# Layer 2's first forget gates set behind the second tile's splitting, and the first experts' last combinations in another order

## The chip, the cores and the metric

The kernel runs on one core of one Trainium2 chip. The metric is the device time of one execution in microseconds (us), the median of three timed runs. One more execution was taken with the hardware profiler; every row quoted here is from it.

## What is computed

The reference sends 256 tokens of width 1024 through two transformer blocks in fp32. The first has two layers (attention, a short convolution), each with a dense feed-forward part. The second has a layer with the HGRN2 mixer and one with stick-breaking attention, each followed by a normalisation over the residual sum, a mixture of 16 experts and another normalisation. What the change touches is the forget gate of the HGRN2 mixer and the output of the first mixture:

```python
def second_block(x, mem, ...):
    ...
    for layer in range(DEPTH):
        ...
            h = x @ a_w_in[layer]
            q, f_raw, i_in, g, qm = jnp.split(h, [...], axis=-1)
            seq_out = hgrn2_mix(q, f_raw, i_in, g, lb_all[layer], a_gnorm[layer])
        ...
        x = post_norm(x, mixed @ w_o[layer], ln_mix_g[layer], ln_mix_b[layer])
        moe_out = hier_moe(x, w_group[layer], b_group[layer], ...)
        x = post_norm(x, moe_out, ln_ffn_g[layer], ln_ffn_b[layer])
    return x

def hgrn2_mix(q, f_raw, i_in, g, lb, gnorm):
    ...
    logf = jnp.logaddexp(jnp.log(lbf), jnp.log1p(-lbf) + jax.nn.log_sigmoid(f_raw))
    kh = -jnp.expm1(logf)
    vh = i_in...
    o = gla_chunkwise(qh, kh, vh, logf)   # S_t = diag(f_t) S_{t-1} + k_t^T v_t ; o_t = q_t S_t
    ...

def hier_moe(x, ...):
    ...                                    # top group, then the top 2 of its 4 experts
    h = jax.nn.silu(einsum('td,edf->tef', xf, w_gate)) * einsum('td,edf->tef', xf, w_up)
    y = einsum('tef,efd->td', h * gates[:, :, None], w_down)
    return y
```

## The kernel before

The 256 tokens are two tiles T of 128 (0 and 1, `x_82` and `x_83` in the order, both x in the trace). A dense product is made of three matmuls in a reduced fp32 format: the weight is split into hi (cast by ScalarE, L506, now and then by VectorE, L502) and lo (subtracted by VectorE, L487), and so is the activation. A weight unit is 128 x 1024 and 512 KB; one tile needs six matmuls of 128 x 512 for it.

Nothing is ordered by hand. A planner runs generators of work (one per tile and side task) against its own clock, and writes out the order of each engine and of the DMA queue. A generator yields what it waits for: a named event, banks of PSUM, free buffers, or a priority. `rS(n)` asks for n of the 34 places of a ring of 128 x 1024 buffers, which holds activations, weights as they come from memory (raw) and their hi and lo. `SMIN` is the number of places that are always counted as taken by activations: `can_dma` lets a new unit be loaded, and `hl_max` lets units be split ahead, only within what is left.

Layer 2 is the projection of HGRN2. For each tile `lhsT` transposes x on TensorE (L464) and splits it; `gemm` takes blocks of 512 columns, and each block has a callback that spends its bank (b0 to b6). b0 and b1 spawn `f_part`, the forget gates: Abs, Exp and Ln on ScalarE (L480, L484), two scalings on VectorE (L498), then Exp and the cast on ScalarE, and the subtraction of the rest on VectorE. The Exp needs its table loaded (L470). b2 spawns `hgrn`, the recurrence: it waits for both parts of the gates, transposes k and q (twelve matmuls, L464), and sets up the decays with products against a constant matrix.

In `moe_task` the experts stand in four groups of slots, q = 0 to 3, and two column halves c. `down(q, c)` is the down product of both tiles, scaled into two buffers (ScalarE L480, VectorE L498). `combined(q, c)` adds it into the tiles' output banks with four matmuls. For q = 3 the two tiles are apart: `down_last(T, c)` (eight matmuls; the trace has two records for each) and `combined_last(T, c)` (two matmuls). Then `moe` takes the statistics of the output bank (L2152), the residual and the gain are applied in four VectorE operations (L498, x<-bk,stat,row), x is transposed, split, and the next layer's product begins. Layer 0 of `moe_task` is the first mixture.

Of the kernel before, what the change touches and what calls it, by code (L numbers as in the profile page):

```python
# [301 lines left out]
class Body:  # L302
# [1092 lines left out]
    def layer2(self, T):  # L1395
        if T == 0:
            self.hv, self.gs, self.ktil = {}, {}, None
            self.SMIN, self.RAWMIN = 19, 2
        yield self.rS(2)
        lhs = self.pair()  # L1400
        ev = self.lhsT(T, self.x[T], lhs, at=self.ut[T])
        lfh = lfl = kk = qq = vv = gs = mm = None
        mix = []

        def a0():
            nonlocal lfh, lfl, kk
            lfh, lfl, kk = self.tS(F32R), self.tS(F32R), self.tS()

        def a1():
            nonlocal qq  # L1410
            qq = self.tS()

        def a3():
            nonlocal vv
            vv = self.hv[T] = self.tS()

        def a4():
            nonlocal gs
            gs = self.gs[T] = self.tS()

        def f_part(acc, c, d, ev, last=True):
            n = d.stop - d.start
            yield self.rH(2)
            t1, t2 = self.tH(), self.tH()
            self.act(t1[:, :n], acc[:, c], AF.Abs)
            self.act(t1[:, :n], t1[:, :n], AF.Exp, scale=-1.0)
            self.act(t1[:, :n], t1[:, :n], AF.Ln, bias=1.0)
            yield self.w()
            self.stt(t2[:, :n], acc[:, c], 0.0, t1[:, :n], ALU.max, ALU.add)
            self.stt(t1[:, :n], acc[:, c], 0.0, t1[:, :n], ALU.min, ALU.subtract)  # L1430
            if last:
                self.free()
            self.act(kk[:, d], t2[:, :n], AF.Exp, scale=-1.0)
            self.scopy(lfh[:, d], t1[:, :n])
            yield self.w()
            self.tt(lfl[:, d], t1[:, :n], lfh[:, d].bitcast(F32), ALU.subtract)
            self.fH(2)
            self.set(ev)

        def b0(acc):  # L1440
            self.sch.spawn(f_part(acc, slice(0, 512), slice(0, 512), f"lf{T}_0"), 0)

        def b1(acc):
            self.scopy(qq[:, :256], acc[:, 256:])
            self.sch.spawn(f_part(acc, slice(0, 256), slice(512, 768), f"lf{T}_1"), 0)

        def b2(acc):
            self.scopy(qq[:, 256:768], acc)
            self.free()
            self.sch.spawn(self.hgrn(T, lfh, lfl, kk, qq, mix), 0)  # L1450

        def b3(acc):
            self.act(vv[:, :512], acc, AF.Copy, scale=128.0 ** -0.5)
            self.free()

        def b4(acc):
            self.act(vv[:, 512:768], acc[:, :256], AF.Copy, scale=128.0 ** -0.5)
            self.set(f"hv{T}")
            self.act(gs[:, :256], acc[:, 256:], AF.Silu)
            self.free()  # L1460

        def b5(acc):
            self.act(gs[:, 256:768], acc, AF.Silu)
            self.free()
            self.set(f"hg{T}")

        def b6(acc):
            nonlocal mm
            qm, mm = self.tH(), self.tH(F32R)
            self.scopy(qm[:, :256], acc[:, :256])  # L1470
            self.free()
            self.sch.spawn(self.mem_attention(T, 0, qm, mm), 0)

        u = self.ids["ain"]
        yield from self.gemm(T, u[:24], lhs, [(b0, 3, a0), (b1, 1, a1), b2, (b3, 1, a3), (b4, 1, a4), b5], ev=ev)
        yield from self.gemm(T, u[24:], lhs, [b6], n=256)
        self.fS(2)
        mix += self.pair()
        self.set(f"mix{T}")
        yield f"hgrn{T}"  # L1480
        yield from self.wo_postnorm(T, 0, mix, mm)
# [477 lines left out]
    def moe_task(self, layer):  # L1959
# [11 lines left out]
        def combine(q, c):  # L1971
            for T in range(2):
                if out[T][c] is None:
                    out[T][c] = self.bank()
                for p in range(2):
                    self.mm(out[T][c], self.selT[:, T * 512 + q * 128:T * 512 + (q + 1) * 128],
                            ys[q, c][p][:, T * 512:(T + 1) * 512], q == 0 and p == 0, False)
            self.fS(2)
# [67 lines left out]
        def down(q, c):  # L2046
            ud = self.ids[f"ed{layer}"][8 * q + 4 * c:8 * q + 4 * c + 4]
            yield [f"hT{layer}_{q}_0", f"hT{layer}_{q}_1", f"gsl{layer}", self.rS(2), self.bk(2)] + [self.unit(u) for u in ud]
            y = [self.bank(), self.bank()]
            ys[q, c] = (self.tS(F32R), self.tS(F32R))  # L2050
            ws = [self.take(u) for u in ud]
            for j in range(2):
                for T in range(2):
                    for e in range(4):
                        self.mm(y[T][32 * e:32 * e + 32], hTs[q][:, T * 256 + j * 128 + 32 * e:T * 256 + j * 128 + 32 * e + 32],
                                ws[e][:, j * 512:(j + 1) * 512], j == 0, j == 1)
            for u in ud:
                self.done(u)
            if c:
                self.fH()  # L2060
            for T in range(2):
                n = slice(T * 512, (T + 1) * 512)
                g = gsl[:, 4 * T + q:4 * T + q + 1]
                self.act(ys[q, c][0][:, n], y[T], AF.Copy, scale=g)
                self.stt(ys[q, c][1][:, n], y[T], g, ys[q, c][0][:, n].bitcast(F32), ALU.mult, ALU.subtract)
                self.free()
            self.set(f"y{layer}_{q}_{c}")

        def down_last(T, c):

            ud = self.ids[f"ed{layer}"][24 + 4 * c:28 + 4 * c]
            yield [f"hT{layer}_3_{T}", f"gsl{layer}", self.bk(1)] + [self.unit(u) for u in ud] + ([] if c else [self.rS(2)])
            y = self.bank()
            if c == 0:
                ys[3, T] = (self.tS(F32R), self.tS(F32R))
            ws = [self.take(u) for u in ud]
            for j in range(2):
                for e in range(4):
                    self.mm(y[32 * e:32 * e + 32], hTs[3][:, T * 256 + j * 128 + 32 * e:T * 256 + j * 128 + 32 * e + 32],
                            ws[e][:, j * 512:(j + 1) * 512], j == 0, j == 1)  # L2080
            if T:
                for u in ud:
                    self.done(u)
            n = slice(c * 512, (c + 1) * 512)
            g = gsl[:, 4 * T + 3:4 * T + 4]
            self.act(ys[3, T][0][:, n], y, AF.Copy, scale=g)
            self.stt(ys[3, T][1][:, n], y, g, ys[3, T][0][:, n].bitcast(F32), ALU.mult, ALU.subtract)
            self.free()
            self.set(f"yl{layer}_{T}_{c}")

        def combined_last(T, c):
            yield f"yl{layer}_{T}_{c}"
            for p in range(2):
                self.mm(out[T][c], self.selT[:, T * 512 + 384:T * 512 + 512], ys[3, T][p][:, c * 512:(c + 1) * 512], False, p == 1)
            self.sch.set(f"moe{layer}_{T}_{c}")
            if c:
                self.fS(2)

        def combined(q, c):
            yield [f"y{layer}_{q}_{c}"] + ([f"selT{layer}_0", f"selT{layer}_1", self.bk(2)] if q == 0 else [])  # L2100
            combine(q, c)
# [10 lines left out]
        for q in range(3):  # L2112
            yield from down(q, 0)
            if q > 1:
                yield from combined(q - 1, 1)
            yield from down(q, 1)
            yield from combined(q, 0)
            if q < 2:
                yield from gate_up(q + 2, (0, 1))
            if q == 0:  # L2120
                yield from combined(0, 1)
                yield from residual(0)
                yield from residual(1)
        self.hold = True
        yield from down_last(0, 0)
        yield from combined(2, 1)
        yield from down_last(0, 1)
        yield from down_last(1, 0)
        yield from combined_last(0, 0)
        yield from combined_last(0, 1)  # L2130
        yield from down_last(1, 1)
        yield from combined_last(1, 0)
        self.fH(2)
# [153 lines left out]
```

## Time and profile before

| | |
|---|---|
| median of three runs | 1202.5 us (1201.07 to 1202.95) |
| the profiled execution | 1199.67 us |
| its span in the trace | 1197.9 us |
| TensorE matmuls busy | 1143.5 us (95%) |
| VectorE busy | 726.8 us (61%) |
| ScalarE busy | 545.9 us (46%) |
| DMA, mean over the span | 252 GB/s |

The span is read from the first to the last instruction in the trace; 1.8 us of the profiled execution lie around it. The busy shares are means over stages with different limits, so a stage is read by itself: in its timeline, the number in brackets behind a row is the idle time of the engine before it, and the name after it is what released the engine. Idle time counts only where the engine that sets the pace has it.

### The profile page before, as it was taken

How to read it: one execution, taken by the hardware profiler on the slowest of the kernel's cores; microseconds unless marked ns; L12 is line 12 of the kernel's file. 1: busy time of each engine (PE TensorE's matmuls, PEld its weight loads, DVE VectorE, ACT ScalarE, POOL GpSimd, SP SyncE). 2: the span in 40 equal slices, each digit the busy share in tenths (PEclk: the TensorE clock that was granted, in tenths of full speed). 3: DMA queues.
4: the chain of work that ended last, by engine and by line, in shares of the span. 5: the costliest groups of instructions: out<-in, count | busy, mean ns of one | idle time of the engine just before them, and what ended most of it. 6: DMA issues, size and time to landing. Idle time of an engine off the chain costs nothing. (4 is left out here: it accounts for less than half of the span.)

```text
span 1197.9 us, 16678 instructions
## 1 busy us (share of the span) xinstructions
PE 1143.5 (95%) x6344; PEld 819.6 (68%) x6344; DVE 726.8 (61%) x1126; ACT 545.9 (46%) x908; POOL 44.7 (4%) x65
## 2 busy tenths in 40 slices
PE   7999989999998999999999999999999899999995
PEld 4777768888886777788887789886333577673331
DVE  4577667667577987665556567768121765564214
ACT  4555465434436455544434484554121456631211
POOL 0021000000000000000000000100000100000001
PEclk9999999999999999999999999999999899999997
DMA  9976768777674966566665332577999742587993
GB/s 373 409 287 248 261 216 293 277 262 257 256 271 137 331 227 211 179 208 202 208 224 179 122 124 71 176 255 280 400 409 409 289 153 75 187 333 311 409 408 148
DMA packets 83544, 301.72 MB, mean 252 GB/s; under 512 B 9408, under 2 KB 9824, under 8 KB 83456
## 3 DMA queue, kind: packets, MB, share of 16 engines
q1 hardware_dynamic: 82224, 298.37, 68.9%
q0 software_dynamic: 944, 1.82, 0.5%
q8 instruction: 52, 0.85, 0.3%
q10 hardware_dynamic: 288, 0.38, 0.1%
q14 instruction: 36, 0.29, 0.1%
HBM read 298.83 MB, written 2.10 MB: 251 GB/s over the span
## 5 line engine op out<-in xcount | busy, mean ns | idle before, releaser
L452 PE MATMUL bk<-hi,tS 128*128 128x512 f32 (+1 forms) x1760 | 586.2, 398 | 14.7 <-ACT hi L506 8.5
L452 PEld LDWEIGHTS bk<-hi,tS 128*128 128x128 f32 x1760 | 331.6, 189 | 87.7 <-ACT hi L506 8.9
L487 DVE TENSOR_TENSOR lo<-raw,hi 128x1024 fp32r<-128x1024 f32 x266 | 317.3, 1221 | 53.3 <-ACT hi L506 51.2
L452 PE MATMUL bk<-lo,tS 128*128 128x512 f32 (+1 forms) x880 | 344.1, 391 | 1.6 <-DVE lo L487 1.6
L506 ACT CAST hi<-raw 128x1024 fp32r<-128x1024 f32 x262 | 263.0, 1049 | 8.5 <-DMA raw<-in_units_dram 7.3
L452 PEld LDWEIGHTS bk<-lo,tS 128*128 128x128 f32 x880 | 167.1, 190 | 34.9 <-DVE lo L487 3.4
L480 ACT ACTIVATE tH<-bk 128x256 f32<-128x256 f32 (+1 forms) x100 | 44.8, 449 | 267.4 <-PE bk L452 267.3
L452 PE MATMUL bk<-hi,tH 128*128 128x512 f32 x384 | 132.6, 395 | 1.4 <-ACT tH L506 1.4
L487 DVE TENSOR_TENSOR tH<-tH,bk 128x256 f32<-128x256 f32 x60 | 25.1, 418 | 144.0 <-ACT tH L480 144.0
L452 PE MATMUL bk<-raw,tB 128*32 128x512 f32 x768 | 92.5, 595 | 0.2 <-DMA raw<-in_units_dram 0.2
L452 PEld LDWEIGHTS bk<-hi,tH 128*128 128x128 f32 x384 | 71.9, 188 | 16.9 <-ACT tH L506 2.1
L452 PE MATMUL bk<-raw,tH 128*32 128x512 f32 x640 | 82.2, 595 | 0.6 <-DMA raw<-in_units_dram 0.5
L452 PE MATMUL bk<-lo,tH 128*128 128x512 f32 x192 | 74.9, 390 | 0.0
L498 DVE SCALAR_TENSOR_TENSOR tS<-raw,cs,tS 128x1024 f32<-128x1024 f32 x52 | 66.5, 1279 | 0.3
L452 PEld LDWEIGHTS bk<-raw,tB 128*32 128x32 f32 x768 | 23.8, 110 | 53.4 <-issue 45.2
L498 DVE SCALAR_TENSOR_TENSOR tS<-bk,gsl,tS 128x512 fp32r<-128x512 f32 x32 | 23.3, 748 | 56.1 <-ACT tS L480 55.8
L464 PE MATMUL bk<-identr,tH 128*128 128x128 f32 x296 | 49.9, 277 | 6.8 <-DVE tH L487 3.0
L452 PEld LDWEIGHTS bk<-raw,tH 128*32 128x32 f32 x640 | 21.6, 109 | 49.6 <-issue 40.2
L464 PEld LDWEIGHTS bk<-identr,tH 128*128 128x128 f32 x296 | 35.8, 140 | 28.7 <-issue 8.8
L480 ACT ACTIVATE tS<-bk,gsl 128x512 fp32r<-128x512 f32 x32 | 21.1, 686 | 61.4 <-PE bk L452 61.4
L506 ACT CAST tH<-bk 128x256 fp32r<-128x256 f32 (+1 forms) x52 | 18.5, 356 | 66.4 <-PE bk L464 63.0
L487 DVE TENSOR_TENSOR tH<-bk,tH 128x256 fp32r<-128x256 f32 (+1 forms) x52 | 20.8, 400 | 45.3 <-ACT tH L506 45.2
(198 smaller groups left out, 994.6 us busy)
## 6 DMA issues: line engine op xcount, KB each, us to landing
raw<-in_units_dram SPq DMA_DIRECT2D x556, 512.0 KB, 5.6
row<-in_rows_dram SPq DMA_DIRECT2D x9, 512.0 KB, 7.8
x<-in_x_dram SPq DMA_DIRECT2D x2, 512.0 KB, 9.0
xsave<-x POOLq DMA_DIRECT2D x2, 512.0 KB, 6.2
out_dram<-x SPq DMA_DIRECT2D x3, 256.0 KB, 2.2
ulv<-in_ulv_dram POOLq DMA_DIRECT2D x1, 384.0 KB, 7.2
cst<-in_consts_dram SPq DMA_DIRECT2D x1, 274.0 KB, 10.9
out_dram<-x ACTq DMA_DIRECT2D x1, 256.0 KB, 2.1
```

Source lines behind the costliest of these rows:

```text
L452: self.nc.tensor.matmul(out, lhsT, rhs, start=start, stop=stop, skip_group_check=shared)
L464: self.nc.tensor.transpose(out, in_, self.ident)
L480: self.nc.scalar.activation(out, in_, func, scale=scale)
L487: self.nc.vector.tensor_tensor(out, a, b, op)
L498: self.nc.vector.scalar_tensor_tensor(out, a, s, b, op0, op1)
L506: self.nc.scalar.copy(out, a)
```

## The change

In layer 2 `SMIN` starts at 13 instead of 19, and goes to 19 when the third block of either tile is done. The forget gates of tile 0 wait for the event `lhs2`, which tile 1 sets when the second half of its x is transposed and split. In the first mixture (layer 0; the second is as before) `combined(2, 0)` goes behind `down_last(0, 0)`, `combined(2, 1)` behind `down_last(0, 1)`, and `down_last(1, 0)` behind both `combined_last` of tile 0.

```diff
     def layer2(self, T):
         if T == 0:
             self.hv, self.gs, self.ktil = {}, {}, None
-            self.SMIN, self.RAWMIN = 19, 2
+            self.SMIN, self.RAWMIN = 13, 2
         yield self.rS(2)
         lhs = self.pair()
         ev = self.lhsT(T, self.x[T], lhs, at=self.ut[T])
+        if T == 1:
+            yield f"{ev}_1"
+            self.sch.set("lhs2")
...
         def f_part(acc, c, d, ev, last=True):
             n = d.stop - d.start
-            yield self.rH(2)
+            yield [self.rH(2)] + (["lhs2"] if T == 0 else [])
...
         def b2(acc):
+            self.SMIN = 19
             self.scopy(qq[:, 256:768], acc)
...
             yield from down(q, 1)
-            yield from combined(q, 0)
+            if q < 2 or layer:
+                yield from combined(q, 0)
...
         yield from down_last(0, 0)
-        yield from combined(2, 1)
+        yield from combined(2, layer)
         yield from down_last(0, 1)
-        yield from down_last(1, 0)
+        if layer:
+            yield from down_last(1, 0)
+        else:
+            yield from combined(2, 1)
         yield from combined_last(0, 0)
         yield from combined_last(0, 1)
+        if layer == 0:
+            yield from down_last(1, 0)
         yield from down_last(1, 1)
```

Where it moves instructions is shown at two places. The first is the start of layer 2. On TensorE, before: bk_5804 is the bank of tile 0's second block, bk_5823 and bk_5830 take tile 1's transposes, bk_5841 is tile 1's first block.

```order
L452 MATMUL bk_5804<-hi_5779,tS_5719 128x512
L464 MATMUL bk_5823<-identr_84,x1_83 128x128 x4
L464 MATMUL bk_5830<-identr_84,x1_83 128x128 x4
L452 MATMUL bk_5841<-hi_5579,tS_5821 128x512
L452 MATMUL bk_5841<-lo_5580,tS_5821 128x512
```

The same place now, with bk_5810 as the bank of tile 0's second block:

```order
L452 MATMUL bk_5810<-hi_5761,tS_5719 128x512
L464 MATMUL bk_5831<-identr_84,x1_83 128x128 x4
L464 MATMUL bk_5838<-identr_84,x1_83 128x128 x4
L452 MATMUL bk_5810<-hi_5779,tS_5718 128x512
L452 MATMUL bk_5810<-lo_5780,tS_5718 128x512
```

Twelve matmuls of tile 0's second block (hi_5779 and hi_5803) now stand between tile 1's transposes and tile 1's first block, which follows as bk_5872. On ScalarE, before: tH_5797 and tS_5736 are tile 0's forget gates, tS_5821 is tile 1's transposed x.

```order
L506 CAST tH_5740<-bk_5737 128x256
L506 CAST hi_5779<-raw_5639 128x1024
L480 ACTIVATE tH_5797<-bk_5744 128x512
L470 ACT_TABLE_LOAD
L480 ACTIVATE tH_5797<-tH_5797 128x512
L484 ACTIVATE tH_5797<-tH_5797,one_108 128x512
L480 ACTIVATE tS_5736<-tH_5798 128x512
L506 CAST tS_5734<-tH_5797 128x512
L506 CAST tS_5821<-bk_5823 128x512
L506 CAST tS_5821<-bk_5830 128x512
L506 CAST hi_5848<-raw_5654 128x1024
```

ScalarE now, where tH_5858 is the forget gates' buffer, tS_5829 tile 1's transposed x, and tS_5809 a copy out of tile 0's second block:

```order
L506 CAST tH_5740<-bk_5737 128x256
L506 CAST hi_5751<-raw_5601 128x1024
L506 CAST hi_5761<-raw_5639 128x1024
L506 CAST hi_5779<-raw_5654 128x1024
L506 CAST hi_5803<-raw_5664 128x1024
L506 CAST hi_5817<-raw_5765 128x1024
L506 CAST tS_5829<-bk_5831 128x512
L506 CAST tS_5829<-bk_5838 128x512
L506 COPY tS_5809<-bk_5810 128x256
L480 ACTIVATE tH_5858<-bk_5744 128x512
L470 ACT_TABLE_LOAD
L480 ACTIVATE tH_5858<-tH_5858 128x512
```

Five weight casts and the two casts of tile 1's x have come before the gates. The second place is the end of the first mixture. On TensorE, before, from `down(2, 1)` and `combined(2, 0)` on (raw is a down product, tS a combination, x_82 tile 0's transposes):

```order
L452 MATMUL bk<-raw,tH 32x512 x16
L452 MATMUL bk<-tS 128x512 x4
L452 MATMUL bk<-raw,tH 32x512 x8
L452 MATMUL bk<-tS 128x512 x4
L452 MATMUL bk<-raw,tH 32x512 x16
L452 MATMUL bk<-tS 128x512 x4
L452 MATMUL bk<-raw,tH 32x512 x8
L452 MATMUL bk<-tS 128x512 x2
L464 MATMUL bk<-identr,x_82 128x128 x8
L452 MATMUL bk<-tS 128x512 x2
```

The same stretch now:

```order
L452 MATMUL bk<-raw,tH 32x512 x24
L452 MATMUL bk<-tS 128x512 x4
L452 MATMUL bk<-raw,tH 32x512 x8
L452 MATMUL bk<-tS 128x512 x8
L452 MATMUL bk<-raw,tH 32x512 x16
L464 MATMUL bk<-identr,x_82 128x128 x8
L452 MATMUL bk<-tS 128x512 x4
```

Tile 0's last combinations (in the eight) now stand ahead of all sixteen matmuls of tile 1's last down product, and tile 1's four last combinations follow the transposes of tile 0. VectorE's row moves with it: there the statistics of tile 0 come after one scaling less, and two of tile 1's scalings stand behind tile 0's x where one stood.

## Rows read from the trace of the kernel before

**Rows 1.** Page, part 1: each engine's busy us, share of the span, instructions.

```profile
PE 1143.5 (95%) x6344; PEld 819.6 (68%) x6344; DVE 726.8 (61%) x1126; ACT 545.9 (46%) x908; POOL 44.7 (4%) x65
```

**Rows 2.** Timeline, TensorE, start of layer 2: start, us, row [idle before <-releaser].

```profile
675.16 1.03 PE L464 MATMUL bk<-identr,x 128*128 128x128 f32 x8
678.57 0.50 PE L452 MATMUL bk<-hi,tS 128*128 128x512 f32 x1 [2.38 <-ACT tS L506]
...
680.09 0.62 PE L452 MATMUL bk<-hi,tS 128*128 128x512 f32 x2
...
680.78 0.40 PE L452 MATMUL bk<-hi,tS 128*128 128x512 f32 x1
```

**Rows 3.** Timeline, ScalarE, the same stretch.

```profile
664.96 1.06 ACT L506 CAST hi<-raw 128x1024 fp32r<-128x1024 f32 x1
672.63 0.60 ACT L480 ACTIVATE tH<-bk 128x512 f32<-128x512 f32 x1 [6.61 <-PE bk L452]
...
677.94 1.07 ACT L506 CAST tS<-bk 128x512 fp32r<-128x512 f32 x2
678.89 2.96 ACT L506 CAST hi<-raw 128x1024 fp32r<-128x1024 f32 x3
```

**Rows 4.** Timeline, VectorE, the same stretch.

```profile
670.59 0.69 DVE L487 TENSOR_TENSOR tH<-bk,tS 128x512 f32<-128x512 f32 x1 [1.75 <-PE bk L452]
...
675.97 1.42 DVE L498 SCALAR_TENSOR_TENSOR tH<-bk,tH 128x512 f32<-128x512 f32 x2 [2.63 <-ACT tH L484]
```

**Rows 5.** Windows: length, busy of each engine (x rows), PEclk, DMA share, GB/s.

```profile
828.00:836.00 8.00, 7.93 (x55) 4.46 (x56) 7.52 (x28) 3.13 (x6) 0.00 (x0) 1.00 0.21 83
838.00:928.00 90.00, 88.11 (x715) 29.74 (x708) 19.87 (x42) 15.13 (x29) 1.08 (x2) 1.00 1.02 404
676.00:680.00 4.00, 1.62 (x7) 0.92 (x6) 2.80 (x5) 3.22 (x6) 0.00 (x0) 1.00 0.00 0
940.00:943.00 3.00, 1.44 (x3) 0.66 (x3) 2.58 (x4) 3.00 (x4) 0.00 (x0) 0.50 1.03 410
```

**Rows 6.** Page, part 6: DMA issues, count, KB each, median us to landing.

```profile
raw<-in_units_dram SPq DMA_DIRECT2D x556, 512.0 KB, 5.6
```

**Rows 7.** Timeline, TensorE, the recurrence of tile 0.

```profile
700.76 1.47 PE L464 MATMUL bk<-identr,tS 128*128 128x128 f32 x12
...
704.76 0.73 PE L452 MATMUL bk<-ulv,tS 128*128 128x512 f32 x2 [0.22 <-ACT tS L480]
```

**Rows 8.** Timeline, ScalarE, where tile 1's forget gates begin.

```profile
685.99 0.60 ACT L480 ACTIVATE tH<-bk 128x512 f32<-128x512 f32 x1 [4.14 <-PE bk L452]
```

**Rows 9.** Timeline, TensorE, end of the first mixture and the next product.

```profile
929.24 3.62 PE L452 MATMUL bk<-raw,tH 128*32 128x512 f32 x26 [0.23 <-DMA raw<-in_units_dram]
...
937.67 0.63 PE L464 MATMUL bk<-identr,x 128*128 128x128 f32 x4 [1.17 <-DVE x L498]
...
941.37 0.79 PE L452 MATMUL bk<-hi,tS 128*128 128x512 f32 x1 [1.09 <-ACT hi L506]
...
943.22 1.05 PE L452 MATMUL bk<-hi,tS 128*128 128x512 f32 x2
...
944.50 1.05 PE L452 MATMUL bk<-hi,tS 128*128 128x512 f32 x2
...
954.01 1.03 PE L464 MATMUL bk<-identr,x 128*128 128x128 f32 x8
```

**Rows 10.** Timeline, VectorE, the same stretch.

```profile
931.90 0.75 DVE L498 SCALAR_TENSOR_TENSOR tS<-bk,gsl,tS 128x512 fp32r<-128x512 f32 x1 [4.37 <-ACT tS L480]
933.62 0.75 DVE L498 SCALAR_TENSOR_TENSOR tS<-bk,gsl,tS 128x512 fp32r<-128x512 f32 x1 [0.97 <-ACT tS L480]
934.29 1.28 DVE L2152 BATCH_NORM_STATS2 tm<-bk 128x6 f32<-128x512 f32 x2
...
938.22 0.75 DVE L498 SCALAR_TENSOR_TENSOR x<-x,stat,row 128x512 f32<-128x512 f32 x1
...
941.35 8.04 DVE L487 TENSOR_TENSOR lo<-raw,hi 128x1024 fp32r<-128x1024 f32 x7 [0.25 <-ACT hi L506]
...
953.24 0.75 DVE L498 SCALAR_TENSOR_TENSOR x<-x,stat,row 128x512 f32<-128x512 f32 x1
```

## The prediction

> **What bounds the kernel now.** The page's first part comes first: TensorE (PE in the rows) is busy 95% of the span [rows 1]. So only what stops TensorE, or slows it, can move the time, and the stages are read for its gaps. The timeline of TensorE shows two places that the change touches. The first is the start of layer 2: the eight transposes of the second tile's input x begin at 675.16, and the next matmul starts at 678.57 after 2.38 us of idle, released by ScalarE's cast of the transposed x [rows 2]. ScalarE's timeline says why the cast is late: from 672.63 it runs the first tile's forget gates (Abs, a table load, Exp, Ln, Exp, a cast), and the casts of the transposes begin only at 677.94, though those transposes were issued from 675.16 on [rows 2, 3]. Before that ScalarE sat idle 6.61 us [rows 3] and VectorE 1.75 and 2.63 us [rows 4]. The second place is the end of the first mixture of experts: TensorE waits for a weight unit at 929.24, then for VectorE's normalised x at 937.67, for ScalarE's cast at 941.37 [rows 9]. The windows add two things: DMA is full there (share 1.02 from 838 to 928) and empty at the first place (0.00), and the granted clock, 1.00 at the first place, is 0.50 from 940 to 943 [rows 5].
>
> **The first tile's forget gates.** What is removed is the queue in front of the two casts. In the new order of ScalarE five weight casts, then the casts of the second tile's transposes, stand ahead of the gates. They begin at 664.96, where one weight cast of 1.06 us stood, so five take until about 670, inside ScalarE's 6.61 us of idle [rows 3]. Of their subtractions on VectorE (1.15 us apiece by 8.04 for seven [rows 10]) three go ahead of 670.59 and two into the 2.63 us before 675.97, where the gates' own steps now are missing [rows 4]; the second tile's residual between them stays. So both engines are free when the transposes end at about 676.2, and the casts run from about 675.8 to 676.9. TensorE has besides twelve matmuls of the first tile's second block behind the transposes, which need only weights already split: 12 x 0.227 = 2.7 us (three in 0.69 us from 680.09 [rows 2]), which covers the casts and the two subtractions. The 2.38 us go, and so does the stutter behind them: six matmuls took 1.52 us from 678.57 to 680.09 where six take 1.36 [rows 2]. Sum: **2.5 us**. All later work in this stage is the same matmuls in another order.
>
> What is late next? The gates: they now start behind a copy that waits for that second block, at about 678.8 instead of 672.63. Behind the copy ScalarE's queue holds the gates and the next weight cast. The gates' first part takes 5.3 us (672.63 to 677.94 [rows 3]) and the half-width second part about half of that, so they end near 687. Who needs them is the recurrence, whose transposes stood at 700.76 [rows 7]; six matmuls (1.36 us) less stand in front of them now, and all is 2.5 us earlier, so about 697: 10 us of cover. ScalarE had 4.14 us of idle before 685.99 [rows 8]; three casts (2.96 [rows 3]) leave this stretch and 5.3 enter, so 1.8 us stay, a little less than the 2.5 us that TensorE is now early. That is the thinnest cover here, and up to 0.7 us could be given back; I take nothing, since the second tile's gates are used far later still.
>
> **The ring places.** Thirteen places are kept free for activations instead of nineteen until the third block, then nineteen again. This lets the extra weight units be split early; it adds no instruction. If a later unit came late for want of a place, TensorE would wait. In the order each unit of this stage is issued at least 120 matmuls ahead of its first use (27 us at 0.227), against a median 5.6 us to land and 2.2 us to split [rows 6, 3, 10]. Cost: nothing, bounded above by one unit's 5.6 + 2.2 = 7.8 us, and I take the lower end since DMA stands at 0.00 there [rows 5]. Does the gain survive the full DMA stretch of the experts? From 828 to 836 DMA is at 0.21, so it had to wait for places [rows 5]; in the order the units wait for the same matmuls as before, so the stream moves forward with TensorE.
>
> **The end of the first experts.** Work is only reordered. Before, the second tile's last down product ran ahead of the first tile's last combination, and its scaling on VectorE (933.62, 0.75 us) stood before the first tile's statistics at 934.29 [rows 10]. In the new order the first tile's last scaling (931.90 to 932.65) is followed at once by the last combining matmuls and the statistics: the first at about 932.6, the second, which needs TensorE's last pair, at about 933.3, so 1.5 us earlier. The start is unchanged, since the unit waited for at 929.24 [rows 9] sets it. The four row operations on x then end at about 937.4 instead of 938.97 [rows 10], and transposes, casts and the first matmul of the next product follow 1.5 us earlier. VectorE has now two of the second tile's scalings behind x where it had one; that delays the first subtraction, so it comes at about 940.1 instead of 941.35 [rows 10], 1.25 us earlier. From it on, TensorE and the second tile's chain (seven subtractions, statistics, x) run as before, since the second tile's last combination has to be done only when its statistics start, behind the seven subtractions (941.35 + 8.04 = 949.39 [rows 10]). I take **1.3 us**; the bounds are 0 (if the four combinations now in a row wait for each other) and 1.5.
>
> [...]
>
> **The sum.** 2.5 + 1.3 = 3.8 us. The profiled execution took 1199.67 us around its span of 1197.9, so the changed one would take 1195.9. The median of the three runs is 1202.5 (1201.07 to 1202.95), 2.8 above the profiled execution; forecast **1198.7 us**.
>
> **Rivals.** *Only one part pays.* Either the recurrence gives the 2.5 us back (ScalarE's cover above is 0.7 us short), or the combinations in a row cost the 1.3. Then 1200.0 to 1201.2. For it: everything after 700 in layer 2 hangs on ScalarE and VectorE as well. Against it: TensorE's waits there are 0.22 us at most up to 712 [rows 7].
>
> [...]
>
> *Slower: the gates are late after all.* [...] For it: a copy that waits for TensorE now stands ahead of them, and ScalarE's cover is thin. Against it: 10 us between the gates' end and their use.
>
> *The change does little.* The gates move but another release of the same cast stands in front (VectorE's five subtractions, 1.15 each, if one waits for its unit): the stall stays, and the experts' end stays bound by DMA, which is full there. Then 1202.5, give or take 1.
>
> **How the numbers follow.** Both parts pay, 0.50 (1197.5 to 1200); one part alone, 0.20; clock up, 0.10; little, 0.08; slower, 0.12. About 0.2% (2.4 us) is what a measurement tells from no change, so faster starts below 1200.1. Faster: the first, the third, and a fifth of the second: 0.62. Same: the rest of the second, the fourth, a little of the first and last: 0.27. Slower: 0.11. The range leaves out most of the slower case and the last of the clock's: 1195.8 to 1203.0.
>
> **What would show it.** Right: no wait of TensorE behind the second tile's transposes at 676; the casts straight behind five weight casts; the recurrence's transposes near 697 without a wait; the first tile's statistics about 1.5 us earlier relative to the unit waited for at 929; the first subtraction 1.25 earlier. Wrong: a new wait on ScalarE's or VectorE's row between 690 and 740; a weight unit waited for in layer 2; the clock at 0.50 in a stretch where it was 1.00; the experts' DMA stretch starting no earlier.

## The result, and the profile after

The changed kernel took 1194.8 us (median of four runs, 1194.35 to 1196.44); the kernel before, measured beside it on the same chip, 1202.7 (1201.07 to 1203.78). The ratio is 0.9944 with a 95% interval of 0.9932 to 0.9956, so 6.7 us less, between 5.3 and 8.2 (the two medians are 7.9 apart, inside that interval). The direction was forecast, the size was not: 3.8 us were forecast, and 1194.8 lies 1.0 under the lower end of the range. Counted by the ratio from the 1202.5 on which the forecast rests, it is 1195.8, that lower end.

In the profiled executions 5.3 us are gone (1199.67 to 1194.35 around spans of 1197.9 and 1192.6). The traced execution of the kernel before was a short one, 3.0 under the median beside which the change was measured; that of the changed kernel is 0.45 under its own. The page's first part still has TensorE at the top, now at 96% against 95% [rows 1]:

```profile
PE 1142.2 (96%) x6344; PEld 820.6 (69%) x6344; DVE 727.1 (61%) x1127; ACT 544.5 (46%) x907; POOL 44.6 (4%) x65
```

To see where the time went, the program is cut at three marks which every kernel of this study has. The first is the start of tile 1's transposes in layer 2 (675.16 before [rows 2]). The second is the last wait of TensorE for a weight unit in the first mixture (929.24 before [rows 9]). The third is a pair of transposes in the next stage, with which the next wait comes that both kernels share; in the kernel before it is this row of TensorE's timeline:

```profile
963.20 0.44 PE L464 MATMUL bk<-identr,tH 128*128 128x128 f32 x2 [0.54 <-ACT tH L506]
```

Stretch A lies between the first two marks, stretch B between the last two. Before, A is 929.24 - 675.16 = 254.08 us and B is 33.96. After, the marks stand at 675.75, 926.44 and 957.85, so A is 250.69 and B 31.41: A gives 3.39, B 2.55, together 5.94. The first mark itself is 0.59 later in the profiled execution of the changed kernel, and the start of the program is the same code; with this, 5.94 - 0.59 is the 5.3 of the span. That mark lies between 675.16 and 677.14 in the twelve traces of this study, so its place says nothing of the change, and stretches are compared from mark to mark.

**Layer 2.** TensorE's timeline of the changed kernel (start, us, row, idle before and its releaser):

```profile
675.75 1.03 PE L464 MATMUL bk<-identr,x 128*128 128x128 f32 x8
676.54 0.48 PE L452 MATMUL bk<-hi,tS 128*128 128x512 f32 x1
...
697.04 1.47 PE L464 MATMUL bk<-identr,tS 128*128 128x128 f32 x12
698.27 3.01 PE L452 MATMUL bk<-ulv,tS 128*128 128x512 f32 x12
701.12 0.40 PE L452 MATMUL bk<-hi,tS 128*128 128x512 f32 x1
```

Behind the eight transposes the next matmul now follows after 0.79 us (675.75 to 676.54), where it took 3.41 us (675.16 to 678.57) with the 2.38 us of idle [rows 2]. The recurrence's transposes start at 697.04, and all twelve products with the constant matrix run in one row at 698.27; before, the last two of them waited at 704.76 [rows 7].

ScalarE's and VectorE's timelines of the same stretch show what stands ahead:

```profile
665.52 4.85 ACT L506 CAST hi<-raw 128x1024 fp32r<-128x1024 f32 x5
676.38 1.07 ACT L506 CAST tS<-bk 128x512 fp32r<-128x512 f32 x2 [6.02 <-PE bk L464]
679.55 0.37 ACT L506 COPY tS<-bk 128x256 f32<-128x256 f32 x1 [2.10 <-PE bk L452]
679.83 0.60 ACT L480 ACTIVATE tH<-bk 128x512 f32<-128x512 f32 x1
...
688.79 0.39 ACT L506 CAST tS<-tH 128x256 fp32r<-128x256 f32 x1
```

```profile
666.61 3.50 DVE L487 TENSOR_TENSOR lo<-raw,hi 128x1024 fp32r<-128x1024 f32 x3 [0.20 <-ACT hi L506]
...
673.84 2.35 DVE L487 TENSOR_TENSOR lo<-raw,hi 128x1024 fp32r<-128x1024 f32 x2
...
690.55 1.02 DVE L487 TENSOR_TENSOR tS<-tH,tS 128x512 fp32r<-128x512 f32 x2
```

Five weight casts fill most of the time in which ScalarE was idle [rows 3], VectorE subtracts three and two units, and at 676.38 ScalarE has nothing else to do than to cast tile 1's transposes. The gates come behind at 679.83. Their last cast on ScalarE ends at 689.2; their last step is VectorE's subtraction of the rest for both parts, which ends at 691.57, and the recurrence that waits for it starts its transposes at 697.04.

**The end of the first mixture.** TensorE's timeline after, from the weight unit waited for:

```profile
926.44 1.90 PE L452 MATMUL bk<-raw,tH 128*32 128x512 f32 x10 [0.23 <-DMA raw<-in_units_dram]
...
934.81 0.63 PE L464 MATMUL bk<-identr,x 128*128 128x128 f32 x4 [0.24 <-DVE x L498]
...
937.06 0.49 PE L452 MATMUL bk<-hi,tS 128*128 128x512 f32 x1 [0.52 <-ACT hi L506]
...
938.36 0.50 PE L452 MATMUL bk<-lo,tS 128*128 128x512 f32 x1 [0.81 <-DVE lo L487]
...
948.41 0.63 PE L464 MATMUL bk<-identr,x 128*128 128x128 f32 x4 [0.46 <-DVE x L498]
949.86 0.63 PE L464 MATMUL bk<-identr,x 128*128 128x128 f32 x4 [0.82 <-DVE x L498]
950.25 0.47 PE L452 MATMUL bk<-hi,tS 128*128 128x512 f32 x1
...
957.85 0.44 PE L464 MATMUL bk<-identr,tH 128*128 128x128 f32 x2 [0.54 <-ACT tH L506]
```

VectorE's timeline of the same stretch:

```profile
929.97 1.29 DVE L2162 BATCH_NORM_STATS2 tm<-bk 128x6 f32<-128x512 f32 x2
...
937.10 8.03 DVE L487 TENSOR_TENSOR lo<-raw,hi 128x1024 fp32r<-128x1024 f32 x7
945.04 1.28 DVE L2162 BATCH_NORM_STATS2 tm<-bk 128x6 f32<-128x512 f32 x2
...
948.97 0.75 DVE L498 SCALAR_TENSOR_TENSOR x<-x,stat,row 128x512 f32<-128x512 f32 x1
```

And the windows behind the mixture's end (length, busy of each engine with its rows, granted clock, DMA share, GB/s):

```profile
940.00:943.00 3.00, 3.00 (x15) 2.49 (x14) 3.00 (x4) 2.70 (x3) 0.00 (x0) 1.00 1.02 406
943.00:946.00 3.00, 3.00 (x15) 2.46 (x14) 3.00 (x4) 0.59 (x1) 0.00 (x0) 1.00 0.82 317
```

Counted from the unit waited for, tile 0's statistics come at 3.53 us (929.97 - 926.44) where they came at 5.05 [rows 9, 10], and the first subtraction at 10.66 where it came at 12.11. The granted clock is 1.00 where it was 0.50 [rows 5]. In its place TensorE has two waits for tile 1's normalised x, 0.46 and 0.82 us, which the kernel before did not have at 954.01 [rows 9].

### The profile page after: what moved, and what is told of

Read it like the earlier page. It is cut to its first block, busy times and chain, and to the rows that moved or that the text cites. A ratio compares the mean times of both kernels' runs of the same rounds, so it can differ in the third digit from the quotient of the medians.

```text
span 1192.6 us, 16678 instructions
## 1 busy us (share of the span) xinstructions
PE 1142.2 (96%) x6344; PEld 820.6 (69%) x6344; DVE 727.1 (61%) x1127; ACT 544.5 (46%) x907; POOL 44.6 (4%) x65
```

## Experiments

Before they ran, two readings stood against each other: that the two parts are independent and each brings what it removes, or that one part carries all and the other's gain is given back later. Beside that, each part had inner questions: which half of the layer 2 edit works, whether the moved steps or the clock make the mixture's gain, and whether more is to be had. Each ratio below is to the kernel before, measured beside it on the same chip. The stretches of the profiled executions, in us:

```
kernel                               A        B
before                            254.08    33.96
after                             250.69    31.41
layer 2 part alone                250.67    34.79
mixture part alone                255.73    31.43
gates behind tile 1's x, alone    254.71    33.83
ring places alone                 255.38    33.64
before with spare matmuls         254.13    32.91
tile 1's last down product alone  256.05    31.31
after, statistics not held back   250.70    31.76
after, second mixture too         250.71    31.42
after, one subtraction on GpSimd  250.82    32.18
after, combinations back          250.83    31.31
```

### The layer 2 part alone

```diff
-            self.SMIN, self.RAWMIN = 19, 2
+            self.SMIN, self.RAWMIN = 13, 2
...
+        if T == 1:
+            yield f"{ev}_1"
+            self.sch.set("lhs2")
...
-            yield self.rH(2)
+            yield [self.rH(2)] + (["lhs2"] if T == 0 else [])
...
         def b2(acc):
+            self.SMIN = 19
```

> Only the layer 2 part of the change (forget gates of tile 0 behind tile 1's splitting, 13 ring places, then 19); the first mixture as before. Theory 1, two independent gains: TensorE's lead behind layer 2 is 3.4 us as in the trace of the changed kernel, and nothing of it is lost or added at the end of the first mixture, so about 3.4 us under before, ratio 0.997; the granted clock falls to 0.50 behind the first mixture as before. Rival, the gain at the first mixture's end hangs on the lead from layer 2: the clock stays at 1.00 there and the kernel is 4.5 to 5.5 us under before, ratio 0.996.

1198.07 us against 1201.96: ratio 0.9966 (0.9952 to 0.998), so 4.1 us less (2.4 to 5.8). A is 250.67, the value of the changed kernel, so the 3.4 us of A belong to this part alone. B is 34.79, not shorter but 0.83 longer than before: the clock falls behind the mixture, as expected (0.58 from 940 to 942, 0.50 to 946). It falls there, to 0.50 over two us or more, in all four traces that keep the old order of the mixture and have no spare matmuls (before, this kernel and the two halves of the layer 2 edit below), and their B lies between 33.64 and 34.79, so B is known to about 1 us where the clock falls.

### The mixture part alone

```diff
-            yield from combined(q, 0)
+            if q < 2 or layer:
+                yield from combined(q, 0)
...
-        yield from combined(2, 1)
+        yield from combined(2, layer)
         yield from down_last(0, 1)
-        yield from down_last(1, 0)
+        if layer:
+            yield from down_last(1, 0)
+        else:
+            yield from combined(2, 1)
         yield from combined_last(0, 0)
         yield from combined_last(0, 1)
+        if layer == 0:
+            yield from down_last(1, 0)
```

> Only the first mixture's combinations moved; layer 2 as before. Theory 1, two independent gains: 2.4 us under before, ratio 0.998, of which some 1.4 from the earlier statistics and 1 from a clock that stays at 1.00 behind the mixture; the 2.38 us wait behind tile 1's transposes in layer 2 stays. Rival, the clock's staying up was chance or hangs on the lead from layer 2: it falls to 0.50 as before and the kernel is 1.3 us under before, ratio 0.999.

1199.26 us against 1201.96: ratio 0.9982 (0.9972 to 0.9991), so 2.2 us less (1.1 to 3.4). B is 31.43, as in the changed kernel. The two parts' gains, 4.1 and 2.2, make 6.3, and both together gave 6.7: within the intervals they add, and neither is seen to take the other's.

A is 1.65 longer than before in this trace, though nothing of it was changed. TensorE's timeline and the window of this kernel's layer 2 show why:

```profile
677.05 1.04 PE L464 MATMUL bk<-identr,x 128*128 128x128 f32 x8
680.46 0.50 PE L452 MATMUL bk<-hi,tS 128*128 128x512 f32 x1 [2.38 <-ACT tS L506]
...
681.18 1.22 PE L452 MATMUL bk<-hi,tS 128*128 128x512 f32 x2
```

```profile
680.00:688.00 8.00, 7.54 (x25) 5.82 (x26) 5.29 (x6) 3.73 (x5) 0.00 (x0) 0.79 0.05 12
```

The same 2.38 us of idle as in [rows 2] are followed here by a mean granted clock of 0.79 over 8 us: the pair of matmuls at 681.18 takes 1.22 us, where the pair at 680.09 takes 0.62 [rows 2]. In the kernel before the same window reads 1.00:

```profile
680.00:688.00 8.00, 8.00 (x37) 6.60 (x36) 3.84 (x4) 3.79 (x6) 0.00 (x0) 1.00 0.35 117
```

### Gates behind tile 1's x, with nineteen places kept

```diff
+        if T == 1:
+            yield f"{ev}_1"
+            self.sch.set("lhs2")
...
-            yield self.rH(2)
+            yield [self.rH(2)] + (["lhs2"] if T == 0 else [])
```

> Only the forget gates' wait for tile 1's splitting; 19 ring places throughout and the first mixture as before, so TensorE has no second-block matmuls behind tile 1's transposes and only one weight cast stands ahead. If the order of the casts on ScalarE is what the 2.38 us wait was about, TensorE waits there only for the casts themselves, 0.3 to 0.6 us, and the kernel is 1.9 to 2.4 us under before, ratio 0.998. If the wait for the ring places was what mattered, it is within 0.5 us of before.

1201.36 us against 1201.96: ratio 0.9996 (0.9987 to 1.0005), no difference. Yet the wait behind the transposes is nearly gone: 0.24 us at 677.93. It is later work that pays it back. Timelines of TensorE and of ScalarE in this kernel's recurrence:

```profile
708.26 1.76 PE L464 MATMUL bk<-identr,tS 128*128 128x128 f32 x12
...
713.73 0.73 PE L452 MATMUL bk<-ulv,tS 128*128 128x512 f32 x2 [1.00 <-ACT tS L480]
```

```profile
711.78 1.28 ACT L470 ACT_TABLE_LOAD   x1
713.08 0.87 ACT L480 ACTIVATE tS<-bk 128x512 f32<-128x512 f32 x2
```

The order of the recurrences has changed: both tiles' transposes and decay products follow each other within 6 us (702.83 and 708.26), where the changed kernel has them 16 us apart (697.04 and 713.27). So ScalarE's four table loads come within 10 us, from 704.48 on, and TensorE waits 1.00 us for the activations behind the third. The expected gain of about 2 us was wrong; the wait had moved.

### Thirteen places kept, gates as before

```diff
-            self.SMIN, self.RAWMIN = 19, 2
+            self.SMIN, self.RAWMIN = 13, 2
...
         def b2(acc):
+            self.SMIN = 19
```

> Only the ring places (13, then 19 from the third block); the forget gates stay ahead of tile 1's casts and the first mixture as before. TensorE now has twelve matmuls (2.7 us) behind tile 1's transposes, but half of them need a weight whose cast stands behind the gates' Ln. If the cover by matmuls is enough by itself, the wait of 2.38 us is gone but for some 0.5 us, and the kernel is about 2 us under before, ratio 0.998. If the order of the casts is needed, the wait comes back behind the twelve matmuls, and the kernel is within 1 us of before.

1201.88 us against 1201.96: ratio 1.0003 (0.9994 to 1.0012), no difference. TensorE's timeline of this kernel:

```profile
679.03 0.50 PE L452 MATMUL bk<-lo,tS 128*128 128x512 f32 x1 [0.39 <-DVE lo L487]
...
697.96 0.50 PE L452 MATMUL bk<-lo,tS 128*128 128x512 f32 x1 [0.76 <-DVE lo L487]
...
714.25 0.73 PE L452 MATMUL bk<-ulv,tS 128*128 128x512 f32 x2 [0.99 <-ACT tS L480]
```

The 2.38 us are gone here too: ScalarE still casts tile 1's x behind the gates' Ln and a weight cast, at 677.62, but with three weights split ahead of them (665.77, 2.96 us) TensorE has matmuls of tile 0's second block to run behind the transposes. It then outruns VectorE's subtractions (0.39 and 0.76), and the recurrence waits 0.99, with both tiles' transposes as close together as in the kernel before this one (703.35 and 708.79). So each half of the edit removes the wait and pays it back in smaller ones. With one more of 0.27 near 741 in both, the idle times seen are 1.5 us there and 2.4 here; what A loses beyond them is not told apart by these runs. Only both halves together, with five units split ahead and the gates behind, leave no wait.

### The kernel before with eight spare matmuls at the mixture's end

```diff
         yield from combined_last(1, 0)
+        yield from spare(4)
...
         yield from combined_last(1, 1)
+        yield from spare(4)
```

> The kernel before, with four spare matmuls of 128 x 512 (some 1 us) that nobody reads behind tile 1's third of four last combinations in the first mixture, and four more behind the fourth, where TensorE waited 1.17 and 1.09 us. If the clock falls there because TensorE stands idle, it now stays at 1.00 from 940 to 948, the matmuls from 943 on are 0.23 us apart instead of 0.43, TensorE waits instead for tile 1's x at 954, whose chain is unchanged, and the kernel is 0 to 1 us under before (0.75 if casting x by halves is worth what it was in the changed kernel), ratio 0.9994. If the clock falls for another reason, the window from 940 stays at 0.50 and the time is that of before within 0.3 us.

Each `spare(4)` multiplies constants into an unused bank. 1201.15 us against 1201.76: ratio 0.9999 (0.9991 to 1.0008). The windows of this kernel, two us each:

```profile
940.00:942.00 2.00, 1.18 (x8) 1.09 (x8) 1.99 (x3) 1.04 (x2) 0.00 (x0) 1.00 1.03 412
942.00:944.00 2.00, 1.40 (x5) 0.56 (x3) 1.59 (x2) 2.00 (x4) 0.00 (x0) 1.00 1.02 406
944.00:946.00 2.00, 1.61 (x7) 1.36 (x8) 2.00 (x3) 2.00 (x4) 0.00 (x0) 1.00 1.04 416
```

The order of every engine is otherwise that of the kernel before, and the clock stays at 1.00, where it fell to 0.50 in all four traces without spare matmuls. That is one trace, and the subtraction on GpSimd below has one in which the clock fell with the waits of the changed kernel, so what lets it fall is not shown. B is 1.05 us shorter (32.91 against 33.96; 0.73 to 1.88 against the four). In the measured times no gain is seen (1.1 less to 1.0 more by the interval); a gain of the trace's size lies at its edge. So the clock's worth stands on the trace alone.

### Only tile 1's last down product moved

```diff
-        yield from down_last(1, 0)
+        if layer:
+            yield from down_last(1, 0)
         yield from combined_last(0, 0)
         yield from combined_last(0, 1)
+        if layer == 0:
+            yield from down_last(1, 0)
```

> Of the first mixture's moves only one: tile 1's last down product behind tile 0's last combinations; both combinations of the third group stay where they were, layer 2 as before. If this one is what brings tile 0's statistics forward, the time is that of the mixture's part alone, some 2.4 us under before, ratio 0.998. If the moved combinations matter by themselves, it is 0.5 us or more behind that.

1199.83 us against 1201.76: ratio 0.9986 (0.9978 to 0.9995), so 1.7 us less. B is 31.31, all of the mixture part's gain, and the clock is 1.00 from 940 to 946. A is 2.0 longer for the same reason as in the mixture part alone: the clock fell behind the 2.37 us of idle in layer 2 (0.79 from 680 to 688).

### The changed kernel with the third group's combinations back in place

```diff
-            if q < 2 or layer:
-                yield from combined(q, 0)
+            yield from combined(q, 0)
...
-        yield from combined(2, layer)
+        yield from combined(2, 1)
         yield from down_last(0, 1)
         if layer:
             yield from down_last(1, 0)
-        else:
-            yield from combined(2, 1)
```

> The changed kernel with the third group's combinations of the first mixture back in their old places; only tile 1's last down product stays behind tile 0's last combinations. If this move alone carries the gain at the mixture's end, the time is that of the changed kernel within 0.3 us, and the stage from the last wait for a weight unit (926.44) to 957.85 takes 31.3 to 31.4 us as there. If the moved combinations carry a part, the stage is 0.3 us or more longer.

1194.87 us against 1201.07: ratio 0.995 (0.9937 to 0.9963). B is 31.31. With the run before this settles it from both sides: the one move of tile 1's last down product carries stretch B, and the moved combinations of the third group carry nothing that can be seen.

### Three tries to gain more

The changed kernel with tile 1's statistics not held back behind the subtractions:

```diff
-            if T == 1 and not self.last[T]:
+            if T == 1 and not self.last[T] and layer:
                 yield lambda: self.tD - 0.3
```

> The changed kernel, with tile 1's statistics behind the first mixture no longer held back: VectorE takes them between the first subtractions, and tile 1's x still behind all seven. In the changed kernel TensorE waits 0.46 and 0.82 us for tile 1's x. If VectorE's chain from the seventh subtraction to x sets that wait, taking the statistics (1.5 us) out of it brings x 1.5 us earlier: 1.0 to 1.4 us under the changed kernel. If the subtractions, now 1.4 us later, hold TensorE instead (0.68 us of matmuls for three, two for one subtraction of 1.15), it is no better than the changed kernel.

1195.57 us against 1201.76: ratio 0.995 (0.9938 to 0.9963), no better than the changed kernel's 0.9944. In TensorE's timeline the waits for tile 1's x are down to 0.29, and a wait for a subtraction stands in their place:

```profile
943.17 0.50 PE L452 MATMUL bk<-lo,tS 128*128 128x512 f32 x1 [0.57 <-DVE lo L487]
...
950.77 0.63 PE L464 MATMUL bk<-identr,x 128*128 128x128 f32 x4 [0.29 <-DVE x L498]
```

VectorE has the same work in the stretch in another order, and TensorE waits for whichever comes later.

The changed kernel with one of VectorE's seven subtractions given to GpSimd:

```diff
-            self.tt(lo, raw, hi.bitcast(F32), ALU.subtract)
+            if i == self.ids["bin"][6]:
+                self.nc.gpsimd.tensor_tensor(lo, raw, hi.bitcast(F32), ALU.subtract)
+                self.chain += 2.9
+            else:
+                self.tt(lo, raw, hi.bitcast(F32), ALU.subtract)
```

> The changed kernel, with the seventh of the subtractions behind the first mixture on GpSimd instead of VectorE. In the changed kernel TensorE waits 0.46 and 0.82 us for tile 1's x, at the end of a chain in which VectorE works without a pause from the first subtraction on. If VectorE's sum is what sets that wait, 1.15 us less of it brings x 1.15 us earlier and the time falls by some 1.1 us, ratio to the changed kernel 0.999. By the two rows of GpSimd on half that size, 1.43 us each, its subtraction takes about 2.9 us from 942.7 on and is done at 945.6, before its matmuls at 946.4. If GpSimd takes over 3.7 us, or slows VectorE beside it, the gain is gone and TensorE waits for that subtraction instead.

1195.56 us against 1201.07: ratio 0.9952 (0.994 to 0.9964), again no better. GpSimd's and VectorE's timelines:

```profile
944.26 3.48 POOL L581 TENSOR_TENSOR lo<-raw,hi 128x1024 fp32r<-128x1024 f32 x1 [9.03 <-ACT hi L506]
947.71 0.55 POOL L521 TENSOR_TENSOR stat<-tm,mhalf 128x1 f32<-128x1 f32 x1
```

```profile
948.28 0.75 DVE L498 SCALAR_TENSOR_TENSOR x<-x,stat,row 128x512 f32<-128x512 f32 x1 [0.51 <-POOL stat L521]
```

GpSimd takes 3.48 us where VectorE takes 1.15, its own small step of the statistics queues behind it at 947.71, and VectorE waits 0.51 for that. B is 0.8 longer than in the changed kernel, but that can't be put down to GpSimd: the clock fell before its subtraction began. Windows of this kernel, and TensorE's first row that comes late:

```profile
934.00:942.00 8.00, 6.44 (x35) 3.66 (x28) 7.96 (x11) 6.74 (x9) 1.23 (x1) 0.91 1.03 408
942.00:950.00 8.00, 8.00 (x32) 6.47 (x31) 7.39 (x12) 2.77 (x4) 5.74 (x5) 0.88 0.63 246
```

```profile
940.77 0.63 PE L452 MATMUL bk<-lo,tS 128*128 128x512 f32 x1
```

Counted from the weight unit waited for (927.94 here, 926.44 there), TensorE's rows ahead of this one are those of the changed kernel within 0.03 us, waits and all; there the granted clock reads 1.00 in both windows, here 0.91 and 0.88, and the three matmuls from 941.20 take 1.28 us where three take 0.68 there (939.40 to 940.08). So moving tile 1's last down product does not keep the clock up in every execution: of the seven traces that have the move (after, the mixture part, the move alone, and the four made from the changed kernel) six show 1.00 behind the mixture and this one does not. With TensorE slower, tile 1's x is no longer waited for. What the subtraction on GpSimd brings with the clock up stays open: one of its six executions took 1192.54 us, under all four of the changed kernel, and five took 1195.5 to 1196.2.

The changed kernel with the same moves in the second mixture:

```diff
-            if q < 2 or layer:
+            if q < 2:
                 yield from combined(q, 0)
...
-        yield from combined(2, layer)
+        yield from combined(2, 0)
...
-        if layer == 0:
-            yield from down_last(1, 0)
+        yield from down_last(1, 0)
```

> The changed kernel with the same moves in the second mixture. At its end the tiles' outputs are what is left to do. If tile 0's statistics come 1.5 us earlier there as in the first mixture and the end hangs on tile 0, the time falls by up to 1.5 us; if the end hangs on tile 1 (the last statistics, x and output of the span are tile 1's) moving tile 1's down product back costs 0.5 to 1.5 us.

1195.64 us against 1201.76: ratio 0.9954 (0.9942 to 0.9967), no better. VectorE's timeline at the end of the program, first this kernel, then the changed one; the first row is tile 0's statistics, the second tile 1's:

```profile
1172.63 1.30 DVE L2158 BATCH_NORM_STATS2 tm<-bk 128x6 f32<-128x512 f32 x2
...
1178.18 1.37 DVE L2158 BATCH_NORM_STATS2 tm<-bk 128x6 f32<-128x512 f32 x2
```

```profile
1175.37 1.28 DVE L2162 BATCH_NORM_STATS2 tm<-bk 128x6 f32<-128x512 f32 x2
...
1178.60 1.38 DVE L2162 BATCH_NORM_STATS2 tm<-bk 128x6 f32<-128x512 f32 x2
```

Tile 0's statistics come 2.7 us earlier, tile 1's 0.4, about what the two executions differ by ahead of it. At the end of the program nothing follows tile 0's row but its output, and the end hangs on tile 1: the move pays only where a next product waits for tile 0.

## Why the prediction came out as it did

**What bounds the kernel** was read rightly: both places named as TensorE's stops gave time, and no other was needed for the 5.94 of the traces (A's part is there 100 us behind the first mark).

**Layer 2, 2.5 forecast, 3.4 measured.** The mechanism held step by step: five weight casts from 665.52 to 670.4 (about 670 forecast), subtractions of three and two units, the casts at 676.38, no wait. The term was mis-sized at two steps. First, the gap was counted by its idle time, 2.38 us, which starts at the end of the transposes' row (675.16 + 1.03 = 676.19); from start to start the matmul comes 3.41 - 0.79 = 2.62 us nearer. With the stutter behind it (forecast 0.16, about 0.3 in the rows) TensorE leads by 2.95 when it enters the recurrence. Second, of the recurrence the prediction said "I take nothing" and feared that 0.7 could be given back. It gave 0.5 more: from the transposes to the first matmul behind the twelve products it takes 701.12 - 697.04 = 4.08 us, where it took 4.57. That ends at the first of these rows of the kernel before:

```profile
705.33 0.40 PE L452 MATMUL bk<-hi,tS 128*128 128x512 f32 x1
```

```profile
700.98 1.05 ACT L506 CAST hi<-raw 128x1024 fp32r<-128x1024 f32 x1
701.92 0.87 ACT L480 ACTIVATE tS<-bk 128x512 f32<-128x512 f32 x2
```

The wait of 0.22 at 704.76 [rows 7] is gone, and 0.27 us around it. In the kernel before a weight cast of 1.05 us stood on ScalarE (700.98) ahead of the activations that lead to those TensorE waited for, and they began 1.16 us behind the transposes (701.92 - 700.76). After, the same unit's cast is VectorE's (697.97, 0.69 us), and the activations begin 0.64 us behind the transposes (697.68). The cover reckoned for the gates held, but was thinner than the forecast 10 us: forecast were 678.8 to 687 with need at 697, measured 679.83 to 689.2 on ScalarE, and the subtraction on VectorE, which the prediction left out, ended at 691.57, 5.5 us before the need at 697.04.

**Ring places, nothing forecast.** No weight unit is waited for in layer 2 of the changed kernel, as forecast. What the prediction did not see is that the places are no mere companion: alone they bring nothing, and without them the gates' move brings nothing.

**First mixture, 1.3 forecast, 2.55 measured.** The reordering itself was sized well: statistics 1.52 earlier from the unit waited for (1.5 forecast), first subtraction 1.45 earlier (1.25 forecast; the four combinations in a row did not hold each other up). The step that failed is "From it on, TensorE and the second tile's chain (seven subtractions, statistics, x) run as before". The chain did, TensorE did not: the granted clock read 1.00 from 940 to 946 where it had read 0.50, and a clock that stays up was given 0.10. TensorE's product takes 1.9 us less (12.41 us from the first matmul's start to the last's before, 10.50 after), but then it waits 0.46 and 0.82 for tile 1's x, since VectorE's chain from the first subtraction to x is as long as ever (937.10 to 949.72 is 12.62; 941.35 to 953.99 was 12.64 [rows 10]). What the faster TensorE still gains comes behind x: it has transposed the first half while VectorE finishes the second, so that the next product starts 0.53 us after x (950.25) where it took 1.29, 0.76 less; the first steps of that product give about 0.3 more. So 1.45 + 0.76 + 0.3 makes the 2.5. In the trace with the spare matmuls the clock's share by itself is 1.05. That it stayed up in the trace of the changed kernel is in part luck: in one of the seven traces with the move it fell.

What sets the clock no run shows. In the trace with the spare matmuls, work without any use, it read 1.00 where it had read 0.50, but the same idle time was not always followed by the same clock, which the last section takes up. The forecast's range leaves room for the clock by an estimate of the author's whose size no run shows; in its place the runs showed B shorter by 1.05 us at 1.00 (the spare matmuls), and A longer by 1.65 and 2.0 us at 0.79 over 8 us of layer 2.

**The sum.** 3.4 + 2.55 is 5.9 in the traces against 3.8 forecast, 0.9 of it in layer 2 and 1.25 at the mixture's end. The measured ratio says 5.3 to 8.2, so 5.9 is inside it. That 6.7 is measured could come from executions of the kernel before in which the clock falls behind the idle in layer 2. Of the four traced kernels that keep the 2.38 us (before, the spare matmuls, the mixture part, the last down product alone), two show the fall (0.79 from 680 to 688), with an A that is 1.65 and 2.0 longer; the eight kernels without that idle read 1.00 from 676 to 688. If half of the executions have it, that is an estimate of 0.9 us more, 6.8 in all. The mean clock of the 59 executions of the kernel before that were measured beside the experiments points the same way: those at 0.988 or less took 1202.0 us (median of 22), those at 0.992 or more 1200.8 (median of 9). Where in the program it fell in them is not on record, so this reason is only argued.

**The rivals.** *Only one part pays* was true of neither part, but of each half of the layer 2 edit. *Gates late* did not come: their cover was 5.5 us. *The change does little* did not come.

## What to carry to other kernels

A wait is worth the distance from start to start, and what stands behind it, not the idle time that a view prints; and removing it can clear the next wait as well. Where two orders depend on each other, as buffer places and the order of steps here, each alone may only move the wait, so a gain has to be followed to a mark far behind the edit. One trace shows one execution: the clock differed between executions of the same rows here (1.00 and 0.79 from 680 to 688), so a gain that hangs on it wants several. Where a stretch reads a low granted clock, as 0.50 here, read in the trace of the change whether it is still low (six traces of seven read 1.00 here), and then which engine's chain stands behind the faster TensorE (VectorE's, with waits of 0.46 and 0.82 us, here).

## What was not expected of the hardware

The same 2.38 us of idle, behind the same instructions, was followed by a granted clock of 1.00 from 680 to 688 in two traces (before, the spare matmuls) and of 0.79 in two others (the mixture part, the last down product alone), with an A longer by 1.65 and 2.0 us. At the end of the first mixture the same rows of TensorE, within 0.03 us over 12.5 us, were followed by 1.00 in one trace (after) and by 0.91 (934 to 942) and 0.88 (942 to 950) in another (the subtraction on GpSimd). With eight spare matmuls of some 0.27 us each the clock read 1.00 from 940 to 946, with TensorE busy 4.19 of the 6 us; behind the mixture it had read 0.50 in four traces without them (from 940 to 946 in the kernel before, TensorE busy 4.44 of 6 us).

An elementwise subtraction of 128x1024 in float32 took 3.48 us on GpSimd and 1.15 us on VectorE, three times as long; GpSimd's own small step of the statistics stood behind it, and VectorE waited 0.51 us for that.
